# Norm products inside a branch bank, branch tile 4 ahead of the first gates, and seven gate products a bank for tiles 2 and 8

## The chip, the cores and the metric

One of the eight cores of a Trainium2 chip runs the whole program in one launch. The metric is device time in microseconds, the median over several executions; smaller is better. The engines are TensorE (PE; its weight loads are PEld), VectorE (DVE), ScalarE (ACT), GpSimd (POOL) and SyncE (SP). They run side by side, each through its own instructions in order, and wait for each other through semaphores.

## What is computed

A trunk of two layers over 1024 prompt frames and 32 frames of a running stream: an RG-LRU layer, and an attention layer over a window. The change lies in the first layer:

```
u = rmsnorm(x, norm_pre) @ w_in
branch, gate = u[..., :D_RNN], u[..., D_RNN:]
conv = conv_b + sum over taps of ext[:, tap:tap + T] * conv_w[tap]
xb = conv.reshape(B, T, N_RG_BLOCKS, RG_BLOCK)
r = sigmoid(einsum('btnc,ncd->btnd', xb, w_r) + b_r)
i = sigmoid(einsum('btnc,ncd->btnd', xb, w_i) + b_i)
log_a = (-LRU_C * r) * softplus(-lam)
a = exp(log_a)
b = sqrt(-expm1(2 * log_a)) * (i * conv)
h = scan of h = a * h + b over time
y = (h * silu(gate)) @ w_out
```

D_RNN is 1408, in 16 gate blocks of 88 channels. D_MODEL is 1024. All in float32.

## The kernel before

**Layout.** Channels lie on the 128 partitions, time on the free axis: 1060 columns (1024, a gap of 3, 32, and one to spare). The 1408 channels are 11 tiles of 128; a tile's columns are worked in three slices of 384, 384 and 292 (`NSA`), each in one PSUM bank. There are eight banks, given out in turn.

**Products in parts.** Each float32 operand is split into a high part rounded to the product's format and a low rest (`split`: ACT makes hi, DVE or, for weights in `LO_POOL`, POOL makes lo). `mm3` multiplies hi by hi, hi by lo and lo by hi into one bank, so a product over eight 128-row blocks is 24 instructions.

**Front.** x is scaled by its gain, split and multiplied by the branch weights before its norm is known. `x_stat` forms the norm's factor per time column in slice n, and writes it into a diagonal matrix (`diag`); `x_norm` spreads it over the partitions with three products on PE (`rs0`, `rs1`, `rs2`, one for each slice; a bank is taken for each), copies it to SBUF on ACT, evacuates the branch banks of tiles 0, 1 and 2 with it on DVE (`branch_evac`), and runs the four-tap convolution (`branch_conv`: one activation on ACT, three DVE instructions, then the split into `chi` and `clo`). `first_mm` issues the branch products of tile m in slice n. In slices 1 and 2 the norm of the slice before stands behind a whole bank.

**Gates.** A gate block of 88 channels doesn't fit tiles of 128. A gate tile needs its own tile's channels and some of its neighbours': with up to 64 such rows in all, they are copied by DMA into one packed tile (`pack_rows`: hi rows from ACT's queue, lo rows from SP's; hi and lo stand under each other, so one product with the hi weights and one with the lo weights do for both). Tiles 2, 4, 6 and 8 have more: the nearer neighbour, with fewer rows, is packed (56 or 64 rows), the other is taken as a native tile (`NATIVE`), with three products of its own. So a bank of `gates` takes 3 + 2 = 5 products, or 3 + 3 + 2 = 8 in those tiles.

**Loop and order.** For t from 0 to 10: the branch products of tile t (from 3 on; 0 to 2 were made in the front), their evacuation and convolution, the gate weights of tile t - 1 (`prep_gate`), `gates` of tile `GATES_AT[t]` (tile 0 at t = 3), the split of conv, the packed rows of tile t - 1, and the recurrence (`recur`). The row buffers of the loop are 24 (`NROW`), the raw weights have four, their hi and lo parts six each. The instructions are put in order by a scheduler, with regions marked `urgent` moved ahead; `pin` keeps one in the order of the program. So the order on each engine is not that of the code.

**Lines in the profile.** L150 to L152 are the three products of `mm3` (banks `br` of the branch, `gt` of the gates, `gb` of the later gate path), L296 the norm's products and L299 ACT's copy of them, L283 to L289 the norm's factors and `diag`, L207 the evacuation into `ext`, L222 and L224 the convolution, L116 and L117 the hi and lo parts of a split, L371 the DMAs of the packed rows, L390 and L391 the products on them, L129 the weight loads.

## Time and profile before

| what | us |
|---|---|
| median of three runs (905.33, 905.42, 906.95) | 905.42 |
| the profiled execution | 905.81 |
| its span, first to last instruction | 904.0 |
| PE, DVE, ACT, POOL busy | 885.4, 708.1, 563.1, 221.7 |
| mean granted clock of PE | 0.995 |

A profile's page gives the busy time of each engine, the span in 40 slices, the DMA queues, the chain of work that ended last, and the costliest groups of instructions. Behind it lies the trace, which answers with every instruction in order of time, with what an engine waited for, and with busy times in chosen stretches. A row of the timeline reads: start, length, engine, line, operation, what is written from what, shapes, count, and in brackets the idle time ahead and who ended it. PE's products overlap in the trace: the time of one in a stream is read from start to start, not from its length.

### The profile page before, as it was taken

To read this page: it belongs to the slowest core of one execution; us is meant where nothing else is said; L and a number is where in the kernel's file an instruction comes from. 1 tells how busy PE (TensorE), PEld (TensorE's weight loads), DVE (VectorE), ACT (ScalarE), POOL (GpSimd) and SP (SyncE) were. 2 spreads that over 40 slices of the span, in tenths; PEclk is the share of its full clock that TensorE was granted. 3 is DMA by queue.
4 is the path that set the end of the run, shared out by engine and by line. 5 is a ranking of instruction groups with operands and counts; after the bars stand their busy time and mean duration, and the time that the engine had idled before them with its cause. 6 is when DMAs were issued, how large, how long until landed. Compare 5 with 4: busy or idle time off the path is not lost. (4 is left out here: it accounts for less than half of the span.)

```text
span 904.0 us, 15787 instructions
## 1 busy us (share of the span) xinstructions
PE 885.4 (98%) x5434; PEld 864.4 (96%) x5434; DVE 708.1 (78%) x1499; ACT 563.1 (62%) x1231; POOL 221.7 (25%) x263
## 2 busy tenths in 40 slices
PE   9989999999999999999999999999999999999997
PEld 8989999999999999999989899999999999999975
DVE  6797878878897654177897847999999989998776
ACT  8748877879454325364663527766767757797661
POOL 5250212114300001126362432122122011202330
PEclk9999999999999999999999999999999999999999
DMA  9522433242533216445545667338338338334884
GB/s 337 204 75 77 135 88 125 81 128 92 181 119 124 89 57 190 146 135 178 163 157 186 210 205 205 98 111 231 96 110 239 103 97 239 121 112 160 281 250 144
DMA packets 95777, 137.35 MB, mean 152 GB/s; under 512 B 16144, under 2 KB 64304, under 8 KB 95696
## 3 DMA queue, kind: packets, MB, share of 16 engines
q1 hardware_dynamic: 86040, 123.30, 43.9%
q10 hardware_dynamic: 9480, 12.49, 4.5%
q8 instruction: 43, 0.70, 0.3%
q0 software_dynamic: 176, 0.54, 0.2%
q14 instruction: 38, 0.31, 0.1%
HBM read 99.28 MB, written 32.13 MB: 145 GB/s over the span
## 5 line engine op out<-in xcount | busy, mean ns | idle before, releaser
L150 PE MATMUL oa<-yh,whi_outa 128*128 128x384 f32 (+1 forms) x264 | 85.8, 326 | 0.0
L151 PE MATMUL gb<-xlo,whi_ina 128*128 128x384 f32 (+1 forms) x264 | 85.6, 324 | 0.0
L152 PE MATMUL gb<-xhi,wlo_ina 128*128 128x384 f32 (+1 forms) x264 | 85.4, 323 | 0.0
L150 PE MATMUL gb<-xhi,whi_ina 128*128 128x384 f32 (+1 forms) x264 | 85.2, 323 | 0.0
L151 PE MATMUL oa<-yl,whi_outa 128*128 128x384 f32 (+1 forms) x264 | 85.1, 323 | 0.0
L152 PE MATMUL oa<-yh,wlo_outa 128*128 128x384 f32 (+1 forms) x264 | 85.1, 323 | 0.0
L616 POOL TENSOR_TENSOR qp<-qp,qp 128x384 f32<-128x384 f32 (+2 forms) x34 | 49.3, 1449 | 138.2 <-ACT qp L614 126.5
L150 PE MATMUL br<-xhi,whi_ina 128*128 128x384 f32 (+1 forms) x240 | 77.8, 324 | 0.0
L151 PE MATMUL br<-xlo,whi_ina 128*128 128x384 f32 (+1 forms) x240 | 77.8, 324 | 0.0
L152 PE MATMUL br<-xhi,wlo_ina 128*128 128x384 f32 (+1 forms) x240 | 77.4, 323 | 0.0
L117 DVE TENSOR_TENSOR wlo_outa<-raw_outa,whi_outa 128x512 fp32r<-128x512 f32 (+1 forms) x60 | 43.7, 742 | 42.7 <-ACT whi_outa L116 42.6
L931 ACT ACTIVATE P<-P,sm 128x257 f32<-128x257 f32 (+1 forms) x132 | 64.3, 490 | 8.0 <-DVE sm L928 7.9
L698 PE MATMUL gB<-xl,whi_g 128*128 128x384 f32 (+1 forms) x192 | 63.0, 328 | 0.0
L698 PE MATMUL gB<-xh,whi_g 128*128 128x384 f32 (+1 forms) x192 | 62.9, 328 | 0.0
L698 PE MATMUL gB<-xh,wlo_g 128*128 128x384 f32 (+1 forms) x192 | 62.6, 326 | 0.0
L116 ACT ACTIVATE whi_outa<-raw_outa 128x512 fp32r<-128x512 f32 (+1 forms) x60 | 35.5, 594 | 41.5 <-PE oa L151 25.1
L224 DVE SCALAR_TENSOR_TENSOR conv<-ext,pa,conv 128x1060 f32<-128x1060 f32 (+2 forms) x51 | 50.2, 1005 | 9.0 <-ACT conv L222 8.6
L928 DVE CUSTOM_DVE_ANT_0 P<-S,mask,nsnk 128x256 f32<-128x256 f32 (+1 forms) x128 | 52.8, 463 | 4.9 <-PE S L926 4.8
L151 PEld LDWEIGHTS oa<-yl,whi_outa 128*128 128x128 f32 x264 | 49.6, 188 | 0.4
L150 PEld LDWEIGHTS oa<-yh,whi_outa 128*128 128x128 f32 x264 | 49.6, 188 | 0.4
L150 PEld LDWEIGHTS gb<-xhi,whi_ina 128*128 128x128 f32 x264 | 49.7, 188 | 0.0
L152 PEld LDWEIGHTS oa<-yh,wlo_outa 128*128 128x128 f32 x264 | 49.7, 188 | 0.0
(301 smaller groups left out, 2894.0 us busy)
## 6 DMA issues: line engine op xcount, KB each, us to landing
raw_ina<-w_in_a SPq DMA_DIRECT2D x44, 256.0 KB, 2.8
raw_outa<-w_out_a SPq DMA_DIRECT2D x40, 256.0 KB, 2.7
raw_ob<-w_out_b SPq DMA_DIRECT2D x32, 256.0 KB, 2.6
qscr<-quadq SPq DMA_DIRECT2D x8, 768.0 KB
Q<-qscr SPq DMA_DIRECT2D x32, 192.0 KB, 4.3
hscr<-u SPq DMA_DIRECT2D x11, 530.0 KB, 3.0
xr<-xr SPq DMA_DIRECT2D x8, 512.0 KB, 10.2
raw_g<-w_in_b SPq DMA_DIRECT2D x16, 256.0 KB, 3.3
```

The costliest lines, as they stand in the source:

```text
L116: pin(S.activation(dst_hi, src, AF.Copy), behind)
L117: (lo_eng or V).tensor_tensor(dst_lo, src, dst_hi.bitcast(F32), op=ALU.subtract)
L150: nc.tensor.matmul(ps, wh, xh, start=i == 0, stop=False)
L151: nc.tensor.matmul(ps, wh, xl, start=False, stop=False)
L152: nc.tensor.matmul(ps, wl, xh, start=False, stop=last and i == n - 1)
L224: V.scalar_tensor_tensor(c, e[:, c0 + k:c1 + k], pa[:, t, k:k + 1], c, op0=ALU.mult, op1=ALU.add)
L616: G.tensor_tensor(sums[0], sums[0], q, op=ALU.add)
L698: nc.tensor.matmul(ps, l, r, start=c == 0, stop=c == 3 * n - 1)
L928: V.tensor_tensor_reduce(pt[:, h, :w], sb[:, (h - h0) * 256:(h - h0) * 256 + w], msk, -0.125, nsnk[:, sk][:, h:h + 1], op0=ALU.add, op1=AL ...
L931: S.activation(pt[:, h, :w + 1], pt[:, h, :w + 1], AF.Exp, bias=nmax[:, h:h + 1], scale=-1.0, accum_out=rsum[:, h:h + 1])
```

## The change

Four things change.

1. `x_norm` for slices 0 and 1 is called from within `mm3`, in the middle of a branch bank, instead of behind the bank. The first product of the second half is pinned, and so is the first one of the next bank.
2. Branch tile 4: the products of its slices 0 and 1, with their evacuation, are issued in the loop at t = 3, ahead of the gates of tile 0; only slice 2 is left at t = 4.
3. Tiles 2 and 8 (`DUAL`), which have 80 rows in the farther neighbour and 56 in the nearer, take seven products a bank instead of eight. The farther tile's hi rows take two products, by hi and by lo weights. Its 80 low rows stand in a first packed tile with 48 hi rows of the nearer one; the second packed tile holds the other 8 hi rows, the 56 low rows, and the 56 hi rows again, which meet the lo weights. Each packed tile takes one product.
4. For those two tiles the weights have eight blocks instead of six; POOL copies 56 rows of low weights into the second packed block, for each of the two gates. Five DMAs fill the packed tiles (three from ACT's queue, two from SP's) instead of two.

```diff
+DUAL = [t for t in range(MR) if NATIVE[t] is not None and PACKED[t][0][2] <= 60]
+
+def _dual(t):
+
+    (s, r0, n), = PACKED[t]
+    (f, f0, m), = [e for e in _neighbours(t) if e[0] != s]
+    k = P - m
+    return [[(f, f0, m, 1), (s, r0, k, 0)], [(s, r0 + k, n - k, 0), (s, r0, n, 1), (s, r0, n, 0)]]
...
-    def mm3(ps, ws, xs, last=True):
+    def mm3(ps, ws, xs, last=True, mid=None, behind=False):
 
         n = len(ws)
         for i, ((wh, wl), (xh, xl)) in enumerate(zip(ws, xs)):
-            nc.tensor.matmul(ps, wh, xh, start=i == 0, stop=False)
+            if mid and i == n // 2:
+                mid()
+            pin(nc.tensor.matmul(ps, wh, xh, start=i == 0, stop=False), behind and i == 0 or mid and i == n // 2)
...
         for m in range(NS):
-            first_mm(n, m)
-            if m == 2 - n:
-                x_norm(n - 1)
+            first_mm(n, m, (lambda: x_norm(n - 1)) if m == 2 - n else None, m == 3 - n)
...
     def prep_gate(t):
-        gw[t] = weights(A["wg"][t], 4 + 2 * (NATIVE[t] is not None), f"gate{t}")
+        w = gw[t] = weights(A["wg"][t], 4 + 2 * (NATIVE[t] is not None) + 2 * (t in DUAL), f"gate{t}")
+        if t in DUAL:
+
+            n = PACKED[t][0][2]
+            for g in range(2):
+                wh, wl = w[6 + g]
+                G.tensor_copy(wh[64:64 + n], wl[64:64 + n])
 
     def pack_rows(t):
 
+        if t in DUAL:
+            pack[t] = []
+            for i, pieces in enumerate(_dual(t)):
+                pk, off = row(f"pack{t}_{i}", F32R, W), 0
+                for s_, r0, n, x in pieces:
+                    (nc.sync if x else nc.scalar).dma_start(pk[off:off + n, :].bitcast(F32), chl[s_][x][r0:r0 + n, :].bitcast(F32))
+                    off += n
+                pack[t].append((pk, off))
+            return
...
-            if NATIVE[t] is not None:
+            if NATIVE[t] is not None and t not in DUAL:
...
-                nc.tensor.matmul(ps, w[2 + g][0][:kp], pk[:kp, c0:c1], start=False, stop=False)
-                nc.tensor.matmul(ps, w[2 + g][1][:kp], pk[:kp, c0:c1], start=False, stop=True)
+                if t in DUAL:
+                    for x in w[4 + g]:
+                        nc.tensor.matmul(ps, x, chl[NATIVE[t]][0][:, c0:c1], start=False, stop=False)
+                    for i, (pk, kp) in enumerate(packed):
+                        nc.tensor.matmul(ps, w[2 + 4 * i + g][0][:kp], pk[:kp, c0:c1], start=False, stop=i == 1)
...
         if t >= NS:
-            branch_evac(t, branch_mm(t))
+            branch_evac(t, branch_mm(t, (2,) if t == 4 else (0, 1, 2)))
         wts.pop(t)
         if t >= NS - 2:
             prep_in(t + 2)
+        if t == 3:
+            branch_evac(4, branch_mm(4, (0, 1)))
```

**The order on PE behind branch tile 3.** In the names, `br3_2` is the bank of branch tile 3, slice 2; `gt0_0_0` the bank of gate tile 0, gate 0, slice 0; the last number is a buffer's. Before:

```order
L152 MATMUL br3_2_736<-xhi7_99,wlo_ina3_4_649 128x292
L150 MATMUL gt0_0_0_799<-chi0_410,whi_gate0_0_654 128x384
L151 MATMUL gt0_0_0_799<-clo0_411,whi_gate0_0_654 128x384
L152 MATMUL gt0_0_0_799<-chi0_410,wlo_gate0_0_655 128x384
L150 MATMUL gt0_0_1_806<-chi0_410,whi_gate0_0_654 128x384
L151 MATMUL gt0_0_1_806<-clo0_411,whi_gate0_0_654 128x384
L152 MATMUL gt0_0_1_806<-chi0_410,wlo_gate0_0_655 128x384
L150 MATMUL gt0_0_2_813<-chi0_410,whi_gate0_0_654 128x292
L150 MATMUL gt0_1_0_821<-chi0_410,whi_gate0_0_654 128x384
```

Eighteen gate products on tile 0's own channels stood there, then 30 products of branch tile 4, and only then the twelve on the packed rows. In the change, the 48 products of `br4_0` and `br4_1` follow `br3_2`, and their end is:

```order
L166 MATMUL br4_1_803<-xhi7_99,wlo_ina4_4_670 128x384
L164 MATMUL gt0_0_0_855<-chi0_398,whi_gate0_0_654 128x384
L165 MATMUL gt0_0_0_855<-clo0_399,whi_gate0_0_654 128x384
L166 MATMUL gt0_0_0_855<-chi0_398,wlo_gate0_0_655 128x384
L424 MATMUL gt0_0_0_855<-pack0_658,whi_gate0_0_654 128x384
L425 MATMUL gt0_0_0_855<-pack0_658,wlo_gate0_0_655 128x384
L164 MATMUL gt0_0_1_862<-chi0_398,whi_gate0_0_654 128x384
```

Tile 0's gates moved behind 48 branch products, and each bank now takes its packed rows at once, the first as the fourth product.

**The order on PE in the front.** `rs0` is the norm of slice 0; `br1_1` and `br2_1` are the banks of branch tiles 1 and 2 in slice 1. Before:

```order
L152 MATMUL br1_1_376<-xhi7_99,wlo_ina1_4_194 128x384
L296 MATMUL rs0_401<-diag_141,ones_66 128x128
L150 MATMUL br2_1_436<-xhi0_92,whi_ina2_0_226 128x384
L151 MATMUL br2_1_436<-xlo0_100,whi_ina2_0_226 128x384
L152 MATMUL br2_1_436<-xhi0_92,wlo_ina2_0_227 128x384
L150 MATMUL br2_1_436<-xhi1_93,whi_ina2_0_226 128x384
L296 MATMUL rs0_401<-diag_141,ones_66 128x128 x2
```

And in the change:

```order
L165 MATMUL br1_1_376<-xlo3_103,whi_ina1_0_187 128x384
L166 MATMUL br1_1_376<-xhi3_95,wlo_ina1_0_188 128x384
L310 MATMUL rs0_389<-diag_141,ones_66 128x128 x3
L164 MATMUL br1_1_376<-xhi4_96,whi_ina1_4_193 128x384
L165 MATMUL br1_1_376<-xlo4_104,whi_ina1_4_193 128x384
```

The three products of `rs0` moved twelve products forward, into the middle of `br1_1`, and stand together; `rs1` moves in the same way into the middle of `br0_2`.

**One bank of gate tile 2 on PE.** `chi1` and `clo1` are the native neighbour, `pack2` the packed rows. Before:

```order
L150 MATMUL gt2_0_0_1153<-chi1_419,whi_gate2_4_794 128x384
L151 MATMUL gt2_0_0_1153<-clo1_420,whi_gate2_4_794 128x384
L152 MATMUL gt2_0_0_1153<-chi1_419,wlo_gate2_4_795 128x384
L390 MATMUL gt2_0_0_1153<-pack2_844,whi_gate2_0_788 128x384
L391 MATMUL gt2_0_0_1153<-pack2_844,wlo_gate2_0_789 128x384
```

And in the change:

```order
L166 MATMUL gt2_0_0_1159<-chi2_416,wlo_gate2_0_843 128x384
L419 MATMUL gt2_0_0_1159<-chi1_407,whi_gate2_4_848 128x384
L419 MATMUL gt2_0_0_1159<-chi1_407,wlo_gate2_4_849 128x384
L421 MATMUL gt2_0_0_1159<-pack2_0_900,whi_gate2_0_842 128x384
L421 MATMUL gt2_0_0_1159<-pack2_1_903,whi_gate2_4_848 128x384
```

The product on `clo1` is gone, and the two on one packed tile became one on each of two.

## The prediction

> **What bounds the kernel now.** I read the page first, then who TensorE waits for, then TensorE in stretches of time, then the front instruction by instruction.

> ```profile
> span 904.0 us, 15787 instructions
> ...
> PE 885.4 (98%) x5434; PEld 864.4 (96%) x5434; DVE 708.1 (78%) x1499; ACT 563.1 (62%) x1231; POOL 221.7 (25%) x263
> ```

> TensorE (PE) is busy 98% of the span. The profiled execution took 905.81 us, 1.8 around its span; the median of the runs is 905.42, 0.4 less. A change is worth what it takes off TensorE's stream, or off its few waits:

> ```profile
> PE gt L150 <- ACT chi L116: 3.6, 1, 3.6
> PE ss_p L158 <- POOL qp L616: 2.2, 1, 2.2
> ```

> The largest is the first product of a gate bank (gt) on chi, 3.6 us, once. The windows below give, after the stretch and its length, the busy time of PE, PEld, DVE, ACT, POOL, then the granted clock, DMA share and GB/s.

> ```profile
> 58.29:61.70 3.41, 0.30 (x2) 0.00 (x0) 3.41 (x7) 1.05 (x3) 1.26 (x1) 1.00 0.00 0
> 61.70:65.11 3.41, 2.92 (x10) 2.92 (x11) 3.41 (x9) 1.78 (x4) 2.32 (x1) 0.50 0.46 129
> 80.00:240.00 160.00, 160.00 (x991) 160.00 (x990) 132.44 (x126) 125.40 (x165) 40.34 (x75) 1.00 0.34 106
> ```

> In the front TensorE stands still, VectorE (DVE) is full, and the clock is halved for one stretch after the wait. From 80 to 240 us, over the rest of the gate loop, TensorE never rests. So the front's wait and the number of products are what this change can move.

> **Term 1, branch tile 4 ahead.** Before, the gates of tile 0 follow branch tile 3 directly; the third slice of chi0 isn't there. TensorE's rows (start, length):

> ```profile
> 57.38 0.33 PE L150 MATMUL gt<-chi,whi_gate 128*128 128x384 f32 x1
> 58.26 0.33 PE L152 MATMUL gt<-chi,wlo_gate 128*128 128x384 f32 x1
> 62.19 0.93 PE L150 MATMUL gt<-chi,whi_gate 128*128 128x292 f32 x2 [3.60 <-ACT chi L116]
> 65.47 0.34 PE L150 MATMUL br<-xhi,whi_ina 128*128 128x384 f32 x1
> 70.51 0.34 PE L152 MATMUL br<-xhi,wlo_ina 128*128 128x384 f32 x1
> 70.97 0.41 PE L390 MATMUL gt<-pack,whi_gate 96*128 96x384 f32 x1
> ```

> What a product takes in the stream I read from tile 2's gates, start to start:

> ```profile
> 95.87 0.34 PE L150 MATMUL gt<-chi,whi_gate 128*128 128x384 f32 x1
> 97.27 0.34 PE L150 MATMUL gt<-chi,whi_gate 128*128 128x384 f32 x1
> 98.68 0.30 PE L150 MATMUL gt<-chi,whi_gate 128*128 128x292 f32 x1
> 99.75 0.34 PE L150 MATMUL gt<-chi,whi_gate 128*128 128x384 f32 x1
> ```

> A bank of eight takes 1.40 us at 384 columns (95.87 to 97.27) and 1.07 at 292, so a product takes 0.175 and 0.134. The 18 gate products from 57.38 (twelve of 384, six of 292) would take 2.1 + 0.8 = 2.9 us and end at 60.28; the branch starts at 65.47. Lost: 5.2 us, of which 3.75 is waiting and 1.43 the half clock. At 70.69 the packed rows are wanted and the product starts at 70.97: 0.3 more. In the changed order 48 branch products of 384 columns stand at 57.38 instead. They need tile 4's weights, whose second half POOL splits in the first row below, by 47.4, ten microseconds ahead; gate1's weights come next, by 49.5.

> ```profile
> 46.10 1.31 POOL L117 TENSOR_TENSOR wlo_ina<-raw_ina,whi_ina 128x512 fp32r<-128x512 f32 x1 [0.26 <-ACT whi_ina L116]
> 47.83 1.68 POOL L117 TENSOR_TENSOR wlo_gate<-raw_gate,whi_gate 128x512 fp32r<-128x512 f32 x1 [0.42 <-ACT whi_gate L116]
> ```

> Their two banks are free by then, so they run at once. **Gain: 5.5 us**, if nothing new waits.

> What waits next is the fourth product of tile 0's gates, on pack0. TensorE reaches it at 57.38 + 48 x 0.175 + 3 x 0.175 = 66.3. Pack0's later half is the transfer that SyncE issues in this row; its landing is the "DMA to landing" of that view, and the third row gives another transfer of SyncE:

> ```profile
> 64.35 0.55 SPq L371 DMA_DIRECT2D pack<-clo  x1
> DMA to landing us min/median/max: 6.5/6.5/6.5
> hscr<-u SPq DMA_DIRECT2D x11, 530.0 KB, 3.0
> ```

> Before, it lands at 64.35 + 6.5 = 70.85, which is what TensorE waited for at 70.97. If it stayed there, the new wait would be 4.6 us. How much sooner is it issued? It needs clo1's last slice, which VectorE makes at the end of this chain:

> ```profile
> 29.73 0.17 DVE L283 TENSOR_SCALAR stat<-stat 128x3 f32<-128x3 f32 x1 [1.84 <-ACT xr L281]
> 31.73 1.49 DVE L207 TENSOR_TENSOR ext<-br,rs 128x384 f32<-128x384 f32 x3 [1.82 <-ACT rs L299]
> 37.01 1.17 DVE L284 TENSOR_TENSOR stat<-stat 128x3 f32<-128x3 f32 x1 [0.99 <-ACT stat L282]
> 62.92 1.19 DVE L117 TENSOR_TENSOR clo<-conv,chi 128x292 fp32r<-128x292 f32 x3
> 26.49 1.05 ACT L281 ACTIVATE xr<-xr 128x1024 f32<-128x1024 f32 x1
> 31.20 0.49 ACT L299 ACTIVATE rs<-rs 128x384 f32<-128x384 f32 x1 [1.50 <-PE rs L296]
> 29.64 0.38 PE L296 MATMUL rs<-diag,ones 128*128 128x128 f32 x2
> ```

> **Term 2, the norm products sooner.** rs0's products move from behind branch 1's bank into its middle: 12 products, 12 x 0.175 = 2.1 us sooner, 27.55 instead of 29.64, and all three stand together, so the 1.5 us from the first to the copy (29.64 to 31.20) shrink to about 0.8. ACT's copy of rs0 goes from 31.2 to about 28.4, behind one square of 1.0 us instead of three; VectorE's first evacuation from 31.73 to about 29.1. VectorE is the full engine from there to 65 us, so its idle time decides. Before: 1.84 + 1.82 + 0.99 = 4.65 us. In the changed order I count 1.2 (until 29.1), 0.9 (conv1 on ACT, behind two squares) and 0.6 (rs1): 2.7. The same work then ends 1.95 us sooner: pack0's transfer is issued at 62.4, not 64.35. These rows by themselves take nothing off TensorE's stream; the number of norm products is the same.

> **The new wait.** From 62.4 the landing lies between 65.4 (3.0 us, no wait) and 68.9 (6.5 us, a wait of 2.6). I take 5.2, nearer to the same transfer's own row: landing 67.6, **wait 1.3 us**. The weight load of raw_ina6, which stood ahead of it on SyncE, now stands behind. Behind the waiting product stand only TensorE's own; ScalarE's first gate tanh starts after it as before. Should the third norm's diagonals be late on VectorE (rs2's products stand 44.8 us in, my count of VectorE gives 44 to 46), TensorE waits there up to 0.8 us, and the wait on pack0 is shorter by as much.

> Does a new wait halve the clock? Four more windows:

> ```profile
> 505.26:508.67 3.41, 2.33 (x16) 1.86 (x14) 3.41 (x9) 0.52 (x1) 2.62 (x3) 1.00 0.04 13
> 508.67:512.08 3.41, 2.72 (x20) 2.72 (x21) 3.41 (x7) 2.72 (x9) 1.31 (x2) 1.00 0.45 171
> 874.07:877.49 3.42, 1.21 (x8) 0.72 (x6) 1.84 (x4) 2.69 (x5) 1.10 (x1) 1.00 0.80 253
> 877.49:880.90 3.41, 3.41 (x9) 2.50 (x8) 3.31 (x8) 1.28 (x4) 0.00 (x0) 0.50 0.82 228
> ```

> A window in which TensorE worked 1.21 us (after the 2.2 us wait of ss_p) was followed by half clock, one with 2.33 was not (505.26 and the row behind it). A wait of 1.3 leaves 2.1 in its window, near the harmless row: I charge nothing, and 1.4 us (the loss measured above) from a wait of 2.2 on. [...]

> **Term 3, seven products a bank.** Tiles 2 and 8 each have 2 gates x 3 banks. Twelve products go, eight of 384 and four of 292 columns: 8 x 0.175 + 4 x 0.134 = **1.95 us**, all in the stretch 80 to 240 where TensorE never rests. A product with 120 rows is charged as one with 112, whose columns set it here. What the tiles add:

> ```profile
> 75.91 0.77 ACTq L371 DMA_DIRECT2D pack<-chi  x1
> 96.92 0.34 PE L390 MATMUL gt<-pack,whi_gate 112*128 112x384 f32 x1
> 73.84 0.66 ACT L116 ACTIVATE whi_gate<-raw_gate 128x512 fp32r<-128x512 f32 x1
> 77.91 0.40 ACT L116 ACTIVATE whi_gate<-raw_gate 128x256 fp32r<-128x256 f32 x1
> 65.48 0.19 POOL L217 COPY convst<-ext 128x3 f32<-128x3 f32 x1 [0.18 <-DVE ext L207]
> ```

> For each, ACT issues two transfers more (2 x 0.77) and splits 256 columns more (0.26): 1.8 us, in front of the recurrence's activations. SyncE issues one more, VectorE splits 256 columns more (about 0.3), POOL copies two blocks of 56x128, each between the 0.19 us of a 128x3 copy and the 1.31 of a 128x512 split. All are charged at nothing: pack2 is issued at 75.9 and first used at 96.92, 21 us later, and ACT has 34.6 us idle from 80 to 240. With that cover gone it would be 3.6 us of ACT, and as much on TensorE at worst. The second packed row per such tile takes one more of 24 row buffers; the order shows waits for transfers that long landed.

> **Sum.** -5.5 + 1.3 - 1.95 = -6.15 us. 905.81 - 6.15 = 899.7 for an execution like the profiled one, **899.3** beside the median. Behind 80 us nothing else changes place except by this; later waits follow TensorE's own results, so they move along.

> **The rivals.**
> - *VectorE isn't sooner, or the landing is slow.* A wait of 2.2 to 2.6 with half clock gives -7.45 + 2.6 + 1.4 = -3.4: 902.0. With nothing won on VectorE the wait is 4.6 plus 1.4: -1.45, 904.0, no change. For it: VectorE is full, and POOL's splits hold it up. Against it: 3.66 us of idle time ahead of the first evacuation, most of which goes.
> - *The front doesn't do what it says downstream:* ACT or VectorE paces the gate loop, and TensorE, 6 us sooner, waits for banks: about 905. For it: ACT 125.4 of 160 busy, and it gets 3.6 more. Against: gate banks are wanted again only a branch tile (8 us or more) later.
> - *Slower.* SyncE's queue takes its turn in order, and the pack transfer stands behind two gate loads that wait for ring buffers:

> ```profile
> 60.93 0.33 SPq L129 DMA_DIRECT2D raw_ina<-w_in_a  x1
> SPq L129 <- POOL wlo_ina L117: 11.0, 1, 11.0
> ```

> Before, such a load held SyncE 11.0 us for a split on POOL. If a load ahead of the pack held it until 68.0, the landing would be 74.5, the wait 8.2 plus 1.4: +2.2, 907.6. It turns to slower by 0.2% when the landing passes 74.1. Against: the loads now ahead need the splits of ina4 and gate1, done by 49.5 before.

> **How the numbers follow.** Forecast (wait 0 to 2.2): 0.68, 898.0 to 900.2. Wait over 2.2 with half clock: 0.16, 901.5 to 903.5. No change (pack0 not sooner, or the gain taken back): 0.12, around 904 to 905. Slower: 0.04. A measurement of this kernel can tell about 0.2%, 1.8 us, from no change. Range 897.3 to 903.5: it leaves out the last two cases, and reaches below the forecast for a front that also loses its half clock elsewhere (the runs shown spread 1.6 us). Faster 0.84, within 0.2% 0.12, slower 0.04.

> **What would show it.** Right: the 3.6 us wait on chi gone; clock 1.00 through 57 to 80 us; rs0's copy near 28.4; one wait of 0 to 2.2 us at tile 0's first packed product, ahead of it the last pack transfer landing near 67.6; 42 products in tile 2's gates, in 6.8 us; 80 to 240 with TensorE full. Wrong: a wait there above 2.2, half clock after it, or new waits of TensorE for gate banks or for tile 2's and 8's packed rows.

## The result, and the profile after

| | before | changed |
|---|---|---|
| median of five runs each, us | 906.95 (905.33 to 908.52) | 900.08 (899.17 to 901.78) |
| ratio, 95% interval | | 0.9931, 0.9914 to 0.9948 |
| profiled execution, its span | 905.81, 904.0 | 901.02, 899.2 |
| PE, DVE, ACT, POOL busy | 885.4, 708.1, 563.1, 221.7 | 880.7, 706.9, 563.4, 227.1 |

By the ratio that is 6.2 us less (4.7 to 7.8). Repeated later (c_after below), six runs of the changed kernel gave 900.52 beside 905.25, a ratio of 0.9948 (0.9932 to 0.9964): 4.7 us less (3.3 to 6.2). The forecast was 6.15 us less. In time it is 900.08 where 899.3 was given. The sum holds, but two of its terms don't: the front brought more than forecast and the gate products less. That the two misses nearly cancel is luck.

TensorE's waits in the changed kernel (engine, line, awaited engine, tile and line; then total, times, longest). These are the ones that bear on the change or answer to lines shown of before:

```profile
PE ss_p L172 <- POOL qp L652: 1.8, 1, 1.8
...
PE gt L164 <- ACT g L427: 0.8, 1, 0.8
```

The wait of 3.6 us on chi is gone, and none for packed rows came in its place. What came is a wait for ScalarE in the gates. The timeline's rows for the places the prediction named, on PE, then SyncE's transfer, then VectorE's last slice of clo:

```profile
32.90 0.34 PE L166 MATMUL br<-xhi,wlo_ina 128*128 128x384 f32 x1
46.75 0.40 PE L310 MATMUL rs<-diag,ones 32*128 32x32 f32 x2 [0.33 <-DVE diag L303]
67.32 0.34 PE L424 MATMUL gt<-pack,whi_gate 96*128 96x384 f32 x1
79.80 0.34 PE L164 MATMUL br<-xhi,whi_ina 128*128 128x384 f32 x1
186.21 0.34 PE L164 MATMUL gb<-xhi,whi_ina 128*128 128x384 f32 x1
204.65 0.40 PE L164 MATMUL gt<-chi,whi_gate 128*128 128x292 f32 x1 [0.84 <-ACT g L427]
215.56 0.30 PE L425 MATMUL gt<-pack,wlo_gate 96*128 96x292 f32 x1
...
60.97 1.42 SPq L398 DMA_DIRECT2D pack<-clo  x1
...
59.52 1.20 DVE L129 TENSOR_TENSOR clo<-conv,chi 128x292 fp32r<-128x292 f32 x3
```

The first packed product of tile 0 (67.32) has no bracket: it waited for nothing. Pack0's last half was issued at 60.97. Two new waits stand in the rows, 0.33 us on the third norm's diagonals and 0.84 us on a tanh at tile 8's gates. Two stretches, the first where before had the half clock (columns as in the prediction's windows):

```profile
60.00:64.00 4.00, 4.00 (x24) 4.00 (x23) 2.02 (x5) 2.08 (x4) 2.45 (x5) 1.00 0.70 168
...
80.00:240.00 160.00, 159.16 (x985) 158.53 (x984) 134.19 (x128) 127.37 (x169) 44.25 (x77) 1.00 0.40 118
```

The front runs at full clock. From 80 to 240 TensorE, which had rested nowhere before, now rests 0.84 us.

Four products that stand in every kernel cut the program into stretches. In the rows above they are 32.90 (the 132nd branch product), 79.80 (tile 5's first), 186.21 (the first of `gb`, the later gate path) and 215.56 (the last gate product, whose end counts). In before they are these:

```profile
32.22 0.34 PE L152 MATMUL br<-xhi,wlo_ina 128*128 128x384 f32 x1
84.26 0.34 PE L150 MATMUL br<-xhi,whi_ina 128*128 128x384 f32 x1
191.60 0.34 PE L150 MATMUL gb<-xhi,whi_ina 128*128 128x384 f32 x1
220.56 0.30 PE L391 MATMUL gt<-pack,wlo_gate 96*128 96x292 f32 x1
```

The same subtraction in the trace of every run below gives this table (us; stretch 2 holds tile 2's gates, stretch 3 those of tiles 8 to 10; the rest goes to the last product; the 31 to 33 us ahead of the 132nd branch product stand in no column):

```
run           1: front   2: tiles 2-7   3: tiles 8-10   rest
before          52.04      107.34          29.26       676.86
c_before        53.17      107.33          29.26       678.16
e1_branch       51.55      107.31          29.27       678.98
e2_norm         48.05      107.39          29.31       675.03
e3_dual         53.09      106.51          29.53       679.89
e4_front        46.90      107.36          29.30       677.06
e5_nonorm       50.54      106.37          29.70       677.31
after           46.90      106.41          29.65       676.99
c_after         46.90      106.42          29.64       675.29
e6_dual2        46.89      106.42          29.24       678.00
e7_pin          47.07      106.42          30.45       677.53
e13_join4       46.93      106.41          28.28       679.04
e14_best        46.51      106.42          28.29       682.04
e15_d2diag      46.51      106.41          29.24       677.63
```

The first three columns repeat within 0.2 us wherever the code in them is the same and the clock isn't halved. They show what the runs' medians, with intervals of some 3 us, can't. The change brings 5.14 us in the front (6.27 against the second trace of before, whose half clock lasted two windows), 0.93 in stretch 2, and loses 0.39 in stretch 3: 5.7 or 6.8 us. The rest of the program differs by 5 us between executions (675.0 to 679.9), with no pattern by edit; in e13_join4 and e14_best it holds a wait that comes with the edit.

### The profile page after: what moved, and what is told of

Same layout as the page of the kernel before. It is cut to its first block, busy times and chain, and to the rows that moved or that the text cites. A ratio compares the mean times of both kernels' runs of the same rounds, so it can differ in the third digit from the quotient of the medians.

```text
span 899.2 us, 15790 instructions
## 1 busy us (share of the span) xinstructions
PE 880.7 (98%) x5422; PEld 859.6 (96%) x5422; DVE 706.9 (79%) x1499; ACT 563.4 (63%) x1231; POOL 227.1 (25%) x267
## 4 chain that ended last, share of the span: by engine, by line
PE 77%; DMA 7%; DVE 7%; ACT 2%; issue 2%; SPq 2%; POOL 1%; POOLq 0%; DVEq 0%; ACTq 0%
PE gB L734 7%; PE gb L165 5%; PE gb L166 5%; PE gb L164 5%; PE oa L165 5%; PE oa L164 5%; PE oa L166 5%; PE br L165 4%; PE br L166 4%; PE br L164 4%; PE rAq L734 4%; PE rBq L734 4%; PE obm L734 4%; PE O L997 3%; PE S L962 3%; PE T L987 3%
## 5 line engine op out<-in xcount | busy, mean ns | idle before, releaser
L652 POOL TENSOR_TENSOR qp<-qp,qp 128x384 f32<-128x384 f32 (+2 forms) x34 | 47.0, 1382 | 140.3 <-ACT qp L650 112.9
L129 DVE TENSOR_TENSOR wlo_outa<-raw_outa,whi_outa 128x512 fp32r<-128x512 f32 (+1 forms) x60 | 43.9, 741 | 42.9 <-ACT whi_outa L128 42.8
L967 ACT ACTIVATE P<-P,sm 128x257 f32<-128x257 f32 (+1 forms) x132 | 64.3, 490 | 8.0 <-DVE sm L964 7.9
L238 DVE SCALAR_TENSOR_TENSOR conv<-ext,pa,conv 128x1060 f32<-128x1060 f32 (+2 forms) x51 | 46.3, 926 | 10.4 <-ACT conv L236 9.9
```

The costliest lines, as they stand in the source:

```text
L129: (lo_eng or V).tensor_tensor(dst_lo, src, dst_hi.bitcast(F32), op=ALU.subtract)
L238: V.scalar_tensor_tensor(c, e[:, c0 + k:c1 + k], pa[:, t, k:k + 1], c, op0=ALU.mult, op1=ALU.add)
L652: G.tensor_tensor(sums[0], sums[0], q, op=ALU.add)
L967: S.activation(pt[:, h, :w + 1], pt[:, h, :w + 1], AF.Exp, bias=nmax[:, h:h + 1], scale=-1.0, accum_out=rsum[:, h:h + 1])
```

## Experiments

Twelve runs follow, each beside runs of before on its chip. The theory: TensorE's two waits in the front, on chi and on pack0, both hang on VectorE's chain, so that the front's two parts need each other; and the 0.8 us at tile 8 come from ScalarE's order. The rival: the parts add up independently, branch tile 4 carrying the front. Three switches undo one part of the change each:

```
A, norm products behind the bank again
-            first_mm(n, m, (lambda: x_norm(n - 1)) if m == 2 - n else None, m == 3 - n)
+            first_mm(n, m)
+            if m == 2 - n:
+                x_norm(n - 1)
B, branch tile 4 in its old place
-            branch_evac(t, branch_mm(t, (2,) if t == 4 else (0, 1, 2)))
+            branch_evac(t, branch_mm(t))
...
-        if t == 3:
-            branch_evac(4, branch_mm(4, (0, 1)))
C, eight products a bank
-DUAL = [t for t in range(MR) if NATIVE[t] is not None and PACKED[t][0][2] <= 60]
+DUAL = []
```

**e1_branch (A and C): branch tile 4 alone.**

> Only branch tile 4 stands ahead of the gates of tile 0; norm products and gate banks as before. Theory A (the parts need each other): VectorE gets no start, so the later half of pack0 is issued near 64.3 us as before and lands 5.2 to 6.5 us later, at 69.5 to 70.8. The first packed product is wanted at 66.3: TensorE waits 3.2 to 4.6 us there, and the clock is halved behind it (1.4). Sum -5.5 + 3.2 to 4.6 + 1.4: -0.9 to +0.5 us, no change that can be measured. Theory B (the parts add up independently, branch tile 4 carries the whole front gain): no wait above 1 us at the packed product, -5.5 us.

Measured: ratio 0.9996 (0.9979 to 1.0013), no change; the front 0.5 us shorter. The row of the first packed product, then pack0's issue:

```profile
68.76 0.63 PE L426 MATMUL gt<-pack,whi_gate 96*128 96x384 f32 x1 [3.28 <-DMA pack<-clo]
...
63.43 0.55 SPq L400 DMA_DIRECT2D pack<-clo  x1
```

A wait of 3.28 us, and the clock was halved behind it, in the window from 68.8 to 72.2. Theory A: the wait on chi is exchanged for one on pack0.

**e2_norm (B and C): the norm products alone.**

> Only the norm products stand in the middle of a bank; branch tile order and gate banks as before. Theory A: VectorE's chain ends 3.4 us sooner as in the changed kernel, so the wait on chi shrinks from 3.6 to about 0.2 us and the clock is not halved at 61.7; but the packed products now stand 16 branch products behind the gates, wanted near 63.3, and pack0 lands near 66.2: a wait of 2 to 3 us there, which may halve the clock. Sum: -5.2 + 0.2 + 2.9 - 0.3 (the old pack wait) + 0.45 (rs2's diagonals) + 0 or 1.4: -2.0 or -0.5 us. Theory B (norm products by themselves take nothing off TensorE's stream, as the prediction put it): wait on chi within 0.5 us of 3.6, time within 0.5 us of before.

Measured: 0.9968 (0.9955 to 0.9981), 2.9 us less; the front 4.0 us shorter. The wait on chi is gone altogether, the clock stays at 1.00, and the packed product waits only 0.47:

```profile
PE gt L424 <- DMA pack<-clo: 0.5, 1, 0.5
```

Both theories miss. B, the prediction's own words that these rows "by themselves take nothing off TensorE's stream", falls outright; A expected too little, since pack0 was issued at 59.92 and landed 4.2 us later.

**e3_dual (A and B): seven products a bank alone.**

> Only the gates of tiles 2 and 8 in seven products a bank. Theory A: 12 products go, -1.95 us, and ScalarE does the square root of tile 7 ahead of the first tanh of tile 8, which makes TensorE wait for a bank there, +1.0: -0.95 us; the front waits 3.6 us on chi and 2.2 us on ss_p as before. Theory B: the products' -1.95 us come out whole, with no wait above 0.3 us between 80 and 240 us. Theory C: the longer splits, copies and transfers of tiles 2 and 8 take it all: 0 or slower, with new waits on packed rows.

Measured: 1.0005 (0.9989 to 1.0022), no change. Stretch 2 is 0.8 us shorter, stretch 3 is 0.27 longer, with a wait of 0.7 us on ScalarE's tanh. The front of this execution had two windows at half clock, as the second trace of before. By the stretches that is theory A with 0.56 us for its 0.95. The medians (1.0 us less to 2.0 more) don't reach B's 1.95 us less, and can't tell A from C.

**e4_front (C): both front parts, no packing.**

> Both front parts, gate banks as before. Theory A: chi wait and half clock at 61.7 go, pack0 lands before it is wanted, rs2 waits 0.45: -5.5 + 0.45 = -5.05 us until 75 us. ScalarE's order at tile 8 is the changed kernel's (square root first); if that order alone makes the bank wait there, +0.8 to 1.0 and the end is -4.1. If the 12 products that went were needed for TensorE to get ahead of ScalarE, no wait: -5.05. Theory B (prediction's rival): ScalarE or VectorE paces the gate loop, and gate banks take back the front's gain in several waits: above -2 us. Either way 1.4 us more go if the half clock at 877 goes with a shorter wait on ss_p.

Measured: 0.9957 (0.9941 to 0.9973), 3.9 us less; front 46.90, the same as in the changed kernel. ScalarE does tile 7's square root ahead of tile 8's tanh here too, and TensorE doesn't wait there (29.30). That is theory A's second case, but the products aren't the only difference: here the square root doesn't wait for its input, as it does for 1.82 us in the changed kernel (shown further down). The gate loop doesn't take the front's gain back.

**e5_nonorm (A): the changed kernel without the norm products' move.**

> The changed kernel with the norm products back behind the bank (branch tile 4 ahead and seven products a bank stay). Theory A (VectorE's earlier chain is what the front's gain rests on): pack0 issued near 63.4 us instead of 61.0, a wait of about 3.3 us at the first packed product and the clock halved for 3.4 us behind it, so 3.3 + 1.4 - 0.45 = 4.2 us slower than the changed kernel: -2 us against before. Theory B (branch tile 4 ahead carries the front, norm products add nothing on TensorE's stream): within 1 us of the changed kernel, -5 to -6.

Measured: 0.9986 (0.9970 to 1.0002), 1.3 us less, not clear of no change; the wait on pack0 is 2.27 us with half clock behind it, the front 3.64 us longer than in the changed kernel. Theory A. The wait is 1.0 us shorter than in e1_branch because the transfer landed 4.18 us after its issue here, and 5.19 there; its issue, counted from the 132nd branch product, is the same (32.18 us).

**c_before and c_after: the two kernels again.**

> The kernel before once more, for a second trace of it. Both theories: time within 0.2% of itself. What is asked of the trace: whether the waits of 0.4 to 0.6 us on P near 785 us and of 0.7 to 1.1 us on v near 517 us, which stand in all traces of edited kernels and are 0.2 to 0.3 us in the first trace of before, come with the edits (theory A: absent again, sum below 0.6 us) or from one execution to the next (theory B: present, sum above 0.8 us). And whether its clock is halved behind ss_p again: if a window with little work is what halves it and the windows lie on a grid that is shifted from one execution to the next, it need not be.

> The changed kernel once more, timed beside the next two. Expected: -6 us against before (-7.5 to -4.5). In its trace the wait of 0.8 us at tile 8's gates (TensorE for ScalarE's tanh) comes again if it follows from ScalarE's order (theory A); it is gone if it was chance (theory B). No wait above 0.5 us at the first packed product of tile 0.

Measured: before 0.9992 (0.9974 to 1.0011) of itself. Its waits on v and P were 0.71, 0.38 and 0.37 us: they come with the execution, theory B. The changed kernel's 0.84 us wait on tanh came again to the hundredth (theory A there), so it is the program's.

**e7_pin: tile 7's square root behind tile 8's tanh.**

```
-        for x in (t,) if t < 8 else (8, 9, 10) if t == 10 else ():
+        for x in (t,) if t < 7 else (8, 9, 10) if t == 10 else ():
...
-        recur(t, gates(t))
+        g = gates(t)
+        if t == 8:
+            recur_2(7)
+        recur(t, g)
...
-        pin(S.activation(u, u, AF.Sqrt), t == 8)
+        pin(S.activation(u, u, AF.Sqrt), t in (7, 8))
```

and tile 8's first tanh pinned too, ahead of it.

> The changed kernel with the square root of tile 7 moved behind the tanh of tile 8's gate banks on ScalarE. Theory A (the two table loads, the wait for VectorE's u and the square root ahead of the first tanh hold the banks): the 0.84 us wait at 203.8 goes, 0.8 to 1.0 us sooner than the changed kernel by the trace's row of tile 9's gates, -7 us against before. Theory B (ScalarE as such paces this stretch, its load only moves): a wait of the same size stands somewhere from 200 to 235 us, and nothing is won.

Measured: 0.9959 (0.9942 to 0.9976). The wait moved and grew:

```profile
209.77 0.40 PE L164 MATMUL gt<-chi,whi_gate 128*128 128x292 f32 x1 [1.78 <-ACT g L427]
...
205.44 1.28 ACT L448 ACT_TABLE_LOAD   x1
206.73 1.09 ACT L448 ACTIVATE u<-u 128x1060 f32<-128x1060 f32 x1
207.84 1.28 ACT L427 ACT_TABLE_LOAD   x1
```

Theory B. Table load, square root, table load: 3.65 us in which ScalarE gives no bank back. With seven products a bank at tile 8, TensorE waits in both places tried among these gates; behind six tanh more, for longer.

**e6_dual2: seven products at tile 2 alone.**

```
-DUAL = [t for t in range(MR) if NATIVE[t] is not None and PACKED[t][0][2] <= 60]
+DUAL = [2]
```

> The changed kernel with seven products a bank at tile 2 alone; tile 8 has eight again. Theory A (ScalarE paces the gates of tiles 8 to 10, so tile 8's shorter banks only turn into waiting): no wait for ScalarE's tanh above 0.3 us there; from the first bank of the big gate to the last gate product 29.3 us as in before (the changed kernel has 29.65), so 0.4 us sooner than the changed kernel: 0 to -0.8 against it, -6 against before. Theory B (tile 8's six products are won and the wait is a separate accident of order): the wait goes, and the products come back: 29.65 - 0.84 + 0.98 = 29.8.

Measured: 0.9950 (0.9930 to 0.9971). No wait on tanh, stretch 3 29.24 us. Theory A: in the changed kernel, tile 8's six saved products bought nothing but waiting, and 0.4 us more. The order on ScalarE differs too, though (further down).

**e13_join4: the square roots of tiles 7 to 10 together, behind all gates.**

```
-        for x in (t,) if t < 8 else (8, 9, 10) if t == 10 else ():
+        for x in (t,) if t < 7 else (7, 8, 9, 10) if t == 10 else ():
...
-        pin(S.activation(u, u, AF.Sqrt), t == 8)
+        pin(S.activation(u, u, AF.Sqrt), t >= 7)
```

and tile 10's last tanh (`r` in `recur_1`) pinned too, ahead of them.

> The changed kernel with the square roots of tiles 7 to 10 together behind all gates on ScalarE, so that no table load (1.28 us each) and no square root (1.09) stand among the tanh of tiles 8 to 10. Theory A (that block of 3.65 us on ScalarE is what TensorE waits for, in the changed kernel as well as where the block was moved behind tile 8's tanh): no wait for tanh above 0.3 us from 195 to 220; first bank of the big gate to last gate product 28.3 to 28.8 us (29.65 in the changed kernel): 0.9 to 1.3 us sooner there. Theory B (tanh and exponential alone, 5.6 us a tile on ScalarE against 4.9 on TensorE, already pace it): a wait of 0.5 us or more stays. Behind it VectorE does tile 7's recurrence later; a new wait for banks or for row buffers behind 216 us would show there.

Measured: 0.9971 (0.9953 to 0.9989). In stretch 3 theory A to the tenth: no wait, 28.28 us, 0.98 less than in before, which is all that six products are worth. Then it was given back, in the first row's wait (the last row is the changed kernel's):

```profile
235.81 0.40 PE L164 MATMUL gb<-xhi,whi_ina 128*128 128x292 f32 x1 [2.59 <-DVE u L542]
...
219.72 3.60 DVE L451 SCALAR_TENSOR_TENSOR g<-g,u 128x1060 f32<-128x1060 f32 x3
...
235.20 1.02 DVE L542 TENSOR_TENSOR u<-gb,rs 128x384 f32<-128x384 f32 x2 [0.47 <-POOL rnnst L456]
...
234.82 1.01 DVE L542 TENSOR_TENSOR u<-gb,rs 128x384 f32<-128x384 f32 x2
```

VectorE has the recurrences of tiles 7 to 10 in one piece there, and begins to empty the `gb` banks at 235.20. Counted from the 132nd branch product (31.63 here, 32.90 in the changed kernel) that is 1.65 us later, while TensorE is 1.3 us ahead; so TensorE waits.

**e14_best: the same, and the third norm's diagonals on ScalarE.**

```
-                V.tensor_scalar(diag[:k, t * P:t * P + k], ident[:k, :k], stat[:k, 3, t:t + 1], None, op0=ALU.mult)
+                d, e, f = diag[:k, t * P:t * P + k], ident[:k, :k], stat[:k, 3, t:t + 1]
+                if n == 2:
+                    S.activation(d, e, AF.Copy, scale=f)
+                else:
+                    V.tensor_scalar(d, e, f, None, op0=ALU.mult)
```

> The same, and the three diagonals of the third norm on ScalarE instead of VectorE. Theory A (VectorE is held up by POOL's splits: three diagonals took 3.75 us there from 42.9): ScalarE, idle near 46 us, makes them in about 0.8 us, TensorE's wait of 0.33 us at rs2 goes, VectorE's chain ends up to 3 us sooner: pack0 issued near 58, no wait there. Theory B (whatever VectorE does in that stretch is held up by POOL as much): clo's last slice no sooner than 59, rs2's wait may go. Time: 0.3 to 0.5 us less than the kernel before it in this list, which only the traces can show.

Measured: 0.9974 (0.9957 to 0.9991). The wait at rs2 is gone and the front is 0.39 us shorter. Pack0's issue, counted from the 132nd branch product (33.45 in this trace), comes 0.4 us sooner than in the changed kernel (61.13 against 33.45, 60.97 against 32.90): theory B for VectorE's chain; what took the time instead is shown in the next section. The bank wait behind the gates stays, 2.3 us, with half clock behind it.

**e15_d2diag: the changed kernel with e6_dual2's line and e14_best's diagonals** (square roots as in the changed kernel).

> The version that the runs point to: both front parts, seven products a bank at tile 2 alone, the third norm's diagonals on ScalarE. Theory A (the gains of the stretches add): from branch 1's twelfth product to tile 4's gates 46.5 us (46.9 in the changed kernel), then 106.4 (106.4), then 29.25 to the last gate product (29.65): 0.8 us less than the changed kernel up to there, and nothing new behind it: -6.5 us against before (-8 to -5), which a timing can hardly tell from the changed kernel. Theory B (as with the square roots moved to the end, what is saved in one stretch is waited for in a later one): a wait on banks or rows from 190 to 460 us takes it back.

Measured: 0.9944 (0.9925 to 0.9963), 5.1 us less, median 900.46. Theory A in every stretch: 46.51, 106.41, 29.24, and no wait for banks up to 460 us. By the stretches it beats the changed kernel by 0.8 us; by the runs the two can't be told apart. On ScalarE the three diagonals take 0.89 us, where VectorE took 3.75 for them in the changed kernel.

## Why the prediction was right, step by step

**The waits of the front: right in sum, put down to the wrong part.** I gave 5.5 us to branch tile 4, with 1.3 of it lost to a new wait on pack0, and nothing to the norm products. Alone, the norm products shorten the front by 4.0 us, and branch tile 4 by 0.5 in e1_branch or 1.5 in e5_nonorm, whose landing was sooner; together they bring 5.14. Within the spread of that landing the two add up, so that the parts need each other isn't shown; what failed is the share. The reason is one I had in the working and didn't follow: chi and pack0 both come out of VectorE's chain. If the chain is earlier, the wait on chi goes whether or not something is put in front of it; if it isn't, branch tile 4 only carries TensorE to the next wait on the same chain. My figure for that case (4.6 us of wait and 1.4 of half clock) was of the right kind; e1_branch measured 3.28 and the half clock.

**VectorE's head start: mis-sized, and by the wrong mechanism.** I took 1.95 us, from idle time saved. Counted from the 132nd branch product, pack0 is issued 4.06 us sooner (64.35 against 32.22, 60.97 against 32.90). In before, from 6.22 us ahead of that product to the end of clo's last slice, first the window, then two of its groups (line, engine, operation, count; busy, mean ns; idle time):

```profile
26.00:64.11 38.11, 34.51 (x220) 34.03 (x220) 32.93 (x65) 22.61 (x46) 14.79 (x17) 0.97 0.34 108
```

```profile
L224 DVE SCALAR_TENSOR_TENSOR conv<-ext,pa,conv 128x384 f32<-128x384 f32 (+1 forms) x27 | 18.5, 727 | 0.4 <-ACT conv L222 0.3
L289 DVE TENSOR_SCALAR diag<-ident,stat 128x128 f32<-128x128 f32 (+1 forms) x7 | 1.6, 274 | 0.0
```

and the same in the changed kernel, with POOL's gate splits:

```profile
26.67:60.72 34.05, 33.72 (x222) 33.48 (x221) 29.57 (x63) 21.45 (x43) 15.14 (x17) 1.00 0.34 111
```

```profile
L238 DVE SCALAR_TENSOR_TENSOR conv<-ext,pa,conv 128x384 f32<-128x384 f32 (+1 forms) x27 | 14.6, 576 | 2.1 <-ACT conv L236 1.9
L303 DVE TENSOR_SCALAR diag<-ident,stat 128x128 f32<-128x128 f32 (+1 forms) x6 | 4.4, 793 | 0.0
...
L129 POOL TENSOR_TENSOR wlo_gate<-raw_gate,whi_gate 128x512 fp32r<-128x512 f32 x2 | 7.4, 3676 | 1.4 <-ACT whi_gate L128 1.4
```

VectorE's idle time there falls by only 0.7 us (5.18 to 4.48). Its busy time falls by 3.4, mostly because the same 27 convolution instructions take 14.6 us instead of 18.5: they meet POOL's splits at other moments. In before, four of them took 1.54 to 1.65 us, each beside a split, and the others 0.51 to 0.62; in the changed kernel none took more than 0.62. (The nine splits into `clo` fall from 5.6 to 4.4 us, and before's stretch holds one 0.5 us split of x more.) In return the diagonals and POOL's gate splits (3.7 us on average instead of 1.6) take longer. I took durations as given when I moved work of VectorE past work of POOL; they weren't.

The same shows where ScalarE makes the third norm's diagonals. In e15_d2diag, over the same stretch, VectorE's convolution is back at its old time:

```profile
L238 DVE SCALAR_TENSOR_TENSOR conv<-ext,pa,conv 128x384 f32<-128x384 f32 (+1 forms) x27 | 18.5, 732 | 1.4 <-ACT conv L236 1.2
```

Four of its instructions take 1.63 to 1.65 us again, in e14_best too. So freeing VectorE of 3.75 us of diagonals brought the issue of pack0 only 0.4 us forward.

**The wait on pack0: expected 1.3 us, found none.** The landing after 5.2 us was right: 5.20 in the changed kernel, so 66.2, and the product comes at 67.32. The issue was sooner by the point above. For the same transfer the other traces show 3.9 to 6.5 us.

**rs2's diagonals: inside its bounds.** 0 to 0.8 us was given, 0.33 came; without that wait the front is 0.39 us shorter (e14_best).

**Seven products a bank: half right.** I took 1.95 us (the terms add up to 1.94), 0.97 for each tile. Tile 2 gives 0.93. Tile 8 gives nothing and costs 0.4. The step that failed is the cover: I wrote that ScalarE has 34.6 us idle from 80 to 240, an average, and that gate banks are wanted again only a branch tile later. Neither holds for the last three gate tiles, between which no branch products stand. From tile 8's first gate product to the last one, ScalarE (the fourth busy time) had 1.0 us idle in before:

```profile
203.17:220.86 17.69, 17.69 (x111) 17.69 (x110) 14.87 (x14) 16.66 (x25) 6.43 (x8) 1.00 0.33 105
```

ScalarE's rows there in the changed kernel:

```profile
201.62 1.09 ACT L448 ACTIVATE u<-u 128x1060 f32<-128x1060 f32 x1 [1.82 <-DVE u L441]
202.72 1.28 ACT L427 ACT_TABLE_LOAD   x1
204.02 1.92 ACT L427 ACTIVATE g<-gt,hb 128x384 f32<-128x384 f32 x4
```

Tile 8's first bank was full at 199.2; its tanh starts at 204.02, four in a row. e13_join4 shows that ScalarE's work between these banks is the cause: without the table loads and the square root there is no wait. What made that work too long is only in part shown, for two things changed with tile 8's banks. Ahead of the square root ScalarE waits 1.82 us for `u`, which POOL begins late. First POOL in the changed kernel, then POOL and ScalarE in e4_front, where the first product of `gb` comes at the same 186.21:

```profile
197.80 2.49 POOL L437 TENSOR_TENSOR u<-a 128x1060 f32<-128x1060 f32 x1
...
194.91 1.95 POOL L437 TENSOR_TENSOR u<-a 128x1060 f32<-128x1060 f32 x1 [6.35 <-ACT a L433]
...
199.79 1.09 ACT L448 ACTIVATE u<-u 128x1060 f32<-128x1060 f32 x1
202.19 1.92 ACT L427 ACTIVATE g<-gt,hb 128x384 f32<-128x384 f32 x4
```

In every kernel with seven products at tile 8, tile 6's recurrence stands later in the engines' order (its scan on VectorE at 194.17 here, 184.83 in e4_front), and POOL copies from that scan before it makes tile 7's `u`. In e4_front and e6_dual2, with eight products at tile 8, that scan stands early again and the square root doesn't wait. TensorE wanted the bank at 203.81. A first tanh 1.82 us sooner would have ended by 202.8, an estimate from these rows: the wait then needn't have come. So e6_dual2 doesn't tell shorter banks from the later `u`.

**What stays open.** The half clock behind the late wait on ss_p (1.4 us) was in both traces of before and in neither of the changed kernel; among the edited kernels it was in e1_branch, e3_dual and e14_best. No run shows that an edit causes it. That POOL and VectorE hold each other up was read from the rows; no run took POOL's splits away. And no run has seven products at tile 8 with tile 6's recurrence in its old place, which would part the two causes of the wait there.

## What to carry to other kernels

When two waits of an engine end on the same producer, price the producer's earlier finish first, and the reordering in front of the waits second: here the first alone brought 4.0 of 5.1 us, the second alone 0.5 to 1.5. An engine's idle share over a loop covers nothing at the loop's end if the mix changes there (here ScalarE had 34.6 of 160 us idle, and 1.0 of the last 17.7); ask there what the consumer of each bank does between two banks, table loads included. And where medians spread by 3 us, time the change by the stretch between two products that stand in every kernel: 0.4 us was plain to see so.

## What the runs showed of the hardware

```profile
460.86:464.27 3.41, 1.74 (x8) 1.08 (x8) 3.41 (x5) 3.16 (x11) 3.25 (x4) 1.00 0.10 38
464.27:467.69 3.42, 3.42 (x11) 3.27 (x12) 3.42 (x12) 0.51 (x2) 0.54 (x1) 0.50 0.31 108
```

and the changed kernel at ss_p:

```profile
871.97:875.38 3.41, 1.70 (x6) 1.24 (x7) 2.27 (x5) 3.13 (x8) 1.10 (x1) 1.00 0.95 278
875.38:878.79 3.41, 3.41 (x16) 2.75 (x15) 3.31 (x7) 0.00 (x0) 0.00 (x0) 1.00 0.79 220
```

In the fourteen traces, from 15 us on and leaving out the window in which the last product ends, every window at full clock with up to 1.5 us of work was followed by half clock (0.30 and 1.21 us in before, 0.49 and 1.32 in c_before, 0.13 and 1.00 in e1_branch, 0.62 in e3_dual, 1.35 in e14_best) and none with 1.8 or more (the least in before and in the changed kernel is 2.15); 1.70 to 1.76 went either way (1.70 in the changed kernel stayed at full clock; 1.72 in e7_pin, 1.74 in e4_front and 1.75 in e1_branch didn't). Ahead of 15 us the changed kernel has one of 1.86 us (4.99 to 8.41) that was followed by half clock. The same wait had half clock behind it in one execution and not in another: one of 2.09 us on ss_p in c_before (1.32 us of work in its window) did, and in e15_d2diag (2.00) it didn't. No run shows what sets the grid or the limit.

In c_before's front a halved window was followed by a second one:

```profile
58.06:61.47 3.41, 0.49 (x3) 0.17 (x1) 3.41 (x6) 1.04 (x2) 1.26 (x1) 1.00 0.00 0
61.47:64.89 3.42, 2.73 (x9) 2.73 (x10) 3.42 (x9) 1.78 (x4) 2.13 (x1) 0.50 0.43 115
64.89:68.31 3.42, 3.42 (x14) 3.42 (x13) 1.58 (x3) 2.37 (x2) 0.85 (x6) 0.50 0.78 222
```

With 2.73 us of work at half clock the next window stayed halved; with 2.92 (in the first trace of before) it didn't. That is the 1.1 us between the two traces' fronts.

**Some instructions of VectorE took longer beside POOL's splits, and some of POOL's splits beside VectorE.** In the fourteen traces the 27 convolution instructions of the front took 0.51 to 0.62 us, or 1.53 to 1.67, and nothing between; the 28 long ones of the 378 all ran beside a split of POOL. The third norm's three diagonals took 0.62 us on VectorE in before, between two splits of POOL:

```profile
40.04 0.62 DVE L289 TENSOR_SCALAR diag<-ident,stat 128x128 f32<-128x128 f32 x3
```

and 3.75 in the changed kernel, beside three of them:

```profile
42.94 3.75 DVE L303 TENSOR_SCALAR diag<-ident,stat 128x128 f32<-128x128 f32 x3
...
42.75 1.42 POOL L129 TENSOR_TENSOR wlo_gate<-raw_gate,whi_gate 128x512 fp32r<-128x512 f32 x1 [1.41 <-ACT whi_gate L128]
44.13 2.52 POOL L129 TENSOR_TENSOR wlo_ina<-raw_ina,whi_ina 128x512 fp32r<-128x512 f32 x2
46.63 5.93 POOL L129 TENSOR_TENSOR wlo_gate<-raw_gate,whi_gate 128x512 fp32r<-128x512 f32 x1
```

From 46.63 on it is POOL's split that is long, 5.93 us where the one at 42.75 took 1.42, beside VectorE's next instructions, eight of the convolution in 4.31 us from 46.62 among them, none of which is long. So the slow one is VectorE in the first of these rows and POOL in the last; what slows it isn't shown.
